# Warming transposes in two parts, another order of linear attention's products, and a price on repeated reads

## The chip, the cores and the metric

The kernel runs on one core of a Trainium2 chip. What is measured is the device time of one execution in microseconds, as the median of several runs. Its engines are TensorE (PE in the rows; its weight loads are PEld), VectorE (DVE), ScalarE (ACT), GpSimd (POOL) and SyncE (SP), which starts the transfers. Each engine works off its own queue of instructions in a fixed order; where it needs what another engine makes, it waits.

## The reference

A trunk of two layers over 512 frames and 16 meta tokens of width 1024, in float32. Each layer norms its input, multiplies it by one wide matrix, runs two groups of heads, gates their outputs and multiplies them by an output matrix. The first layer has sparse attention (an indexer scores all keys, the best are picked, softmax over them) and gated linear attention; the second has retention and stick-breaking attention. What matters here is gated linear attention, in chunks of 64:

```python
bcum = jnp.cumsum(log_a, axis=3)
q_t = q * jnp.exp(bcum);  k_t = k * jnp.exp(-bcum)
att = jnp.where(causal, jnp.einsum('bhncd,bhnsd->bhncs', q_t, k_t), 0.0)
o_intra = jnp.einsum('bhncs,bhnse->bhnce', att, v)
contrib = jnp.einsum('bhncd,bhnce->bhnde', k * jnp.exp(b_last - bcum), v)
def step(S, inp):
    dec, con = inp
    return S * dec[..., None] + con, S
o_inter = jnp.einsum('bhncd,bhnde->bhnce', q_t, S_before)
return from_chunks(o_intra + o_inter)
```

Retention has the same form with a fixed decay per head. Its output is also a sum of a product of attention with values and a product of queries with the state before the chunk.

## The kernel before

The kernel doesn't issue its instructions as its code stands. It records them all (one helper, line 406, issues each of them, so every row of the trace has that line, and groups are told apart by the names of their tiles). Each recorded operation gets a price (`price`, with cases by engine and size), and `order` (from line 291) then places them one after the other: for each engine, of what is ready, it takes the operation that could start soonest, with the deadline as the second key, and notes its start and end by the plan's own clock. Constants of the class add what a hand-over between engines costs (`LAT`) and how far neighbours overlap (`OVER`). The order found in that way is the order in each queue. What runs is the same set of instructions whatever the plan's numbers are, but they may stand in another order.

A tile is a whole for the order of its uses: a write into one part of a PSUM tile waits for a read of another part that was recorded ahead of it.

At the start, `consts` (line 675) makes the identity on GpSimd, and 46 transposes of it (`WARM`, line 496) go into one PSUM tile, `y`, whose contents nobody reads. `load_x` (line 737) loads the input in blocks, takes the sum of squares of each, and makes from the norm weights, loaded into `mid`, the tile `gains` by a transpose and a copy on ScalarE. The norm's scale is an exponential of a logarithm on tiles called `tiny`; a block `pt` is scaled by it, turned, and split into a high and a low part (`hh`, `hl`), as are the weights (`raw` to `wh`, `wl`). Three products `hh wh`, `hl wh`, `hh wl` summed in `acc` make one product of full precision.

In the first layer, the in-projection, the indexer's scores, the top-k search and four heads of gated linear attention (`gla_steps`, line 1340) share the time from about 80 to 197 us. The search runs on VectorE in rounds of a maximum of eight (MAX8) and a replacement (MATCH_REPLACE8) over rows `lt` of 272, 400 and 528 keys. A head of linear attention makes an attention tile `att` (masked from PSUM), turned keys `kt`, a small tile `m` (an `x` in the rows) for the meta tokens, with the masked copy `attm` and the copy `ktm` of their turned keys, then the state in seven steps on VectorE (`st<-st,lt,x`), and the output into a `y` tile: for each of four blocks one product of attention and values (`y<-gv,wt`) and one of queries and state (`y<-st,st`). Retention (`retention_steps`, from line 1570) ends in the same way.

Of the kernel before, what the change touches and what calls it, by code (L numbers as in the profile page):

```python
# [16 lines left out]
P = 128  # L17
DM = 1024
KT = DM // P
NMETA = 16  # L20
SEQ = 512
T = NMETA + SEQ
NB = SEQ // P
# [15 lines left out]
def blk(b):  # L39
    return slice(NMETA + P * b, NMETA + P * (b + 1))  # L40
# [126 lines left out]
class Recorder:  # L167
# [48 lines left out]
    def price(self, o):  # L216
        o.mm, o.port = None, False
        n = max([x.free() for x in o.ins + o.outs] or [1])
        sbuf = not any(x.tile.psum for x in o.ins)
        scalar = 65 if any(isinstance(x, View) and x.free() == 1 for x in o.ins) and n > 1 else 0  # L220
        if o.eng == "tensor":
            lhs, rhs = (o.args[1], o.args[2]) if len(o.args) > 2 else (o.kw["lhsT"], o.kw["rhs"])
            turn = o.name == "transpose"
            plain = rhs.dtype == F32
            k, m, n = lhs.shape[0], lhs.free(), rhs.free()
            two = plain and not turn
            o.mm = (32 if k <= 32 else 64 if k <= 64 else P, plain, max(n * 0.45 * (2 if two else 1) + 4, 107 * m / P + 4) + (107 if two and n <= P else 0))
            o.cost = max(273, 170 + 0.4375 * n) if not two else 180 + 1.62 * n
        elif o.eng == "scalar":
            o.cost = (205 if sbuf else 165) + 0.83 * n + (80 if isinstance(o.kw.get("bias"), View) or isinstance(o.kw.get("scale"), View) else 0)  # L230
            if "accum_out" in o.kw:
                o.cost += 200
        elif o.eng == "vector":
            o.port = sbuf and o.name not in ("max", "match_replace")
            if o.name == "tensor_tensor_scan":
                o.cost = 144 + 2.1 * n
            elif o.name in ("tensor_scalar", "tensor_copy") and sbuf:
                o.cost = 160 + 0.52 * n + scalar
            elif o.name == "memset":
                o.cost = 100 + 0.3 * n  # L240
            else:
                o.cost = 148 + 1.05 * n + scalar
            if o.name == "tensor_tensor_reduce" or "accum_out" in o.kw:
                o.cost += 80
            if o.name == "match_replace":
                o.cost += 70
        elif o.eng == "gpsimd":
            o.cost = {"memset": 92 + 0.84 * n, "tensor_tensor": 178 + 2.17 * n}.get(o.name, 194 + 1.5 * n)
        else:
            x = o.outs[0] if o.outs else o.ins[0]  # L250
            kb = n * x.shape[0] / 256
            o.cost = kb * 3.6


    LAT = {"tensor": 55, "vector": 33, "scalar": 34, "gpsimd": 60, "sync": 27}
    OVER = {"vector": -84, "scalar": -103, "gpsimd": -60}
    SWITCH, ROWS = 80, 95
    MARGIN = 300
    STAY = 2000
# [26 lines left out]
    def order(self):  # L286
# [10 lines left out]
        wire = 0.0  # L297
        begun = {}
        result = []

        def ready(o):
            est = 0.0
# [13 lines left out]
        while left:  # L316
            best = None
            for e, xs in lists.items():
                pick = None
                base = free[e] + (last.mm[2] if e == "tensor" and last is not None else 0)  # L320
                for o in xs:
                    est = o.est
                    ok = True
                    for t in o.tiles:
                        if t.slot:
                            continue
                        k = t.kind
                        if t.at != k.next or not k.free:
                            ok = False
                            break  # L330
                        est = max(est, min(k.free)[0] + self.LAT[e])
                    if not ok:
                        continue
                    now = free[e] + (self.slot(last, o) if e == "tensor" and last is not None else 0)
                    start = max(est, now)
                    pri = o.pri
                    if e == "tensor" and last is not None:
                        pri -= self.STAY if o.mm[0] == last.mm[0] else 0
                    key = (max(est + (self.MARGIN if e == "tensor" else 0) - base, 0.0), pri)
                    if pick is None or key < pick[0]:  # L340
                        pick = (key, start, o)
                if pick and (best is None or pick[1] < best[1]):
                    best = pick
            assert best, "no instruction can be placed"
            _, start, o = best
            e = o.eng
            lists[e].remove(o)
            cost = o.cost
            if e == "vector" and o.port and begun.get("pool", (0, 0))[0] < start < begun.get("pool", (0, 0))[1] - 100:
                cost += begun["pool"][1] - start - 70  # L350
            if e == "gpsimd" and begun.get("port", (0, 0))[0] < start < begun.get("port", (0, 0))[1] - 100:
                cost += begun["port"][1] - start - 100
            end = start + cost
            if e == "vector" and o.port:
                begun["port"] = (start, end)
            ends[o] = end
            o.begin, o.end = start, end
            if e == "tensor":
                free[e], last = start, o
            elif e == "sync":  # L360
                free[e] = start + 430
                wire = end = max(wire, start + 1900) + o.cost
                if o.outs and o.outs[0].tile.whole and o.ins and o.ins[0].tile.whole:
                    end = start + 6900
                ends[o] = o.end = end
            else:
                free[e] = end + self.OVER[e]
                if e == "gpsimd":
                    begun["pool"] = (start, end)
            for t in o.tiles:  # L370
                k = t.kind
                if not t.slot:
                    t.slot = min(k.free)
                    k.free.remove(t.slot)
                    k.next += 1
            for t in o.tiles:
                t.left -= 1
                t.ends = max(t.ends, end)
                if not t.left:
                    t.kind.free.append((t.ends, t.slot[1]))  # L380
            result.append(o)
            left -= 1
            for q in o.succs:
                q.wait -= 1
                if not q.wait:
                    ready(q)
# [23 lines left out]
class Kernel:  # L410
# [82 lines left out]


    XL, XC, XN, XW, PW, PL = 2, 9, (0, 1, 1, 2), (1, 4, 7, 10, 13), 0, 0
    WARM = 46

    LAG = {"a": 5, "d": 6, "t": 1, "v": 4, "n": 9, "s": 6, "k": 11}
    TOPY = 3
# [173 lines left out]
    def consts(self):  # L673
        nc, ins = self.nc, self.ins
# [1 line left out]
        self.ident = self.cp.tile([P, P], F32, name="ident")  # L676
        make_identity(nc.core, self.ident.real)

        warm = self.pv()
        for _ in range(self.WARM):  # L680
            self.transpose(warm[:, :P], self.ident)
        self.one = self.cp.tile([P, 1], F32, name="one")
        nc.vector.memset(self.one, 1.0)
        self.eps = self.cp.tile([P, 1], F32, name="eps")
# [2 lines left out]
        self.gains = self.cp.tile([P, 18], F32, name="gains")  # L687
        self.g = self.gains[:, :16].rearrange("p (l k) -> p l k", l=2)
        self.gb = self.gains[:, 16:18]

    def late_consts(self):
        nc, ins = self.nc, self.ins
# [35 lines left out]
    def load_x(self):  # L728
        nc, ins = self.nc, self.ins
# [59 lines left out]
        t = self.tr()  # L789
        self.transpose(t[:, :18], rows)  # L790
        nc.scalar.copy(self.gains, t[:, :18])
        self.split_next()
        todo = [(g, t0, k, c) for g, t0, c in ((first, 0, self.HALVES[0]), (second, T0, self.HALVES[1]))
                for k in range(KT)]
# [545 lines left out]
    def gla_steps(self, head, r, v, gates, ep, qs, ks, kh):  # L1340
        nc = self.nc
# [17 lines left out]

        m = self.tr()  # L1360
        nc.tensor.matmul(m[:NMETA, 0:16], ks[:, :NMETA], qs[:, :NMETA], start=True, stop=True)
        nc.vector.copy_predicated(attm[:NMETA], self.tri[:NMETA, :NMETA], m[:NMETA, 0:16])
        self.transpose(m[:NMETA, 384:512], kh[:, :NMETA])
        ktm = self.ktm[head % 2][:, :64]
        nc.vector.tensor_copy(ktm[:NMETA], m[:NMETA, 384:448])
        yield self.LAG["t"]
# [21 lines left out]
        o = self.pv()  # L1388
        ov = o.rearrange("p (b e) -> p b e", b=NB)
        for b in range(NB):  # L1390
            c = slice(P * b, P * (b + 1))
            nc.tensor.matmul(ov[:, b], att[:, b], vt[:, c], start=True, stop=False)
            nc.tensor.matmul(ov[:, b], qs[:, blk(b)], ss[:, c], start=False, stop=True)
        on = self.head_norm(ov, P, False)
        yield self.LAG["n"]
        while not gates:
# [170 lines left out]
    def retention_steps(self, head, r, v, gates, q, k, qx, kz, kzm, turned):  # L1567
# [27 lines left out]
        o = self.pv()  # L1595
        ov = o.rearrange("p (b e) -> p b e", b=NB)
        for b in range(NB):
            c = slice(P * b, P * (b + 1))
            nc.tensor.matmul(ov[:, b], av[:, b], vt[:, c], start=True, stop=False)
            nc.tensor.matmul(ov[:, b], qx[:, c], ss[:, c], start=False, stop=True)  # L1600
        on = self.head_norm(ov, P, True)
        yield self.LAG["n"]
        while not gates:
# [213 lines left out]
```

## Time and profile before

| | us |
|---|---|
| median of 3 runs | 649.36 (649.32 to 649.61) |
| profiled execution | 648.98 |
| its span, first to last instruction | 647.2 |
| TensorE busy | 625.5 (97%) |
| VectorE busy | 478.3 (74%) |
| ScalarE busy | 402.2 (62%) |

The span is what the rows are counted in; 1.78 us of the profiled execution lie outside it. Busy shares are means over the whole span, and the stages differ: which engine is the bound has to be read stage by stage, and at a waiting instruction the row names what it waited for.

### The profile page before, as it was taken

What the parts mean: (1) busy time and instruction counts of PE and PEld (TensorE: products, weight loads), DVE (VectorE), ACT (ScalarE), POOL (GpSimd) and SP (SyncE); (2) the same over time, 40 slices, a digit from 0 to 9 for tenths busy, and PEclk for the clock granted to TensorE, in tenths of its full rate; (3) what the DMA queues carried; (4) which work ended last, traced back from release to release, by engine and by line L of the source; (5) the groups of instructions that cost most, each with busy time, mean ns of one, the idle gap of its engine ahead of it and who ended that gap; (6) DMA issues with size and microseconds to landing.
All of it is one profiled execution on the core that took longest, in us unless ns stands there. A gap on an engine that the chain in (4) does not pass through costs nothing.

```text
span 647.2 us, 12268 instructions
## 1 busy us (share of the span) xinstructions
PE 625.5 (97%) x4469; PEld 578.9 (89%) x4469; DVE 478.3 (74%) x1110; ACT 402.2 (62%) x904; POOL 80.5 (12%) x199
## 2 busy tenths in 40 slices
PE   7999999899899999999999999999999999999995
PEld 6879999789889999999899999889898888988884
DVE  5777799999997676769532864789945689957443
ACT  5656572352344877789643674899744699946234
POOL 5001101100000112113121210000300010400030
PEclk9899999999999999999999999999999999999999
DMA  8437323222323322112153363212322203224503
GB/s 251 93 95 227 75 64 84 57 78 68 81 65 84 100 66 83 51 50 81 50 149 101 103 208 89 60 33 85 81 82 66 81 2 113 71 79 147 162 18 130
DMA packets 91104, 59.26 MB, mean 92 GB/s; under 512 B 7314, under 2 KB 81628, under 8 KB 91044
## 3 DMA queue, kind: packets, MB, share of 16 engines
q1 hardware_dynamic: 91044, 58.48, 31.4%
q8 instruction: 35, 0.57, 0.4%
q14 instruction: 25, 0.20, 0.1%
HBM read 53.18 MB, written 6.90 MB: 93 GB/s over the span
## 4 chain that ended last, share of the span: by engine, by line
PE 71%; DVE 15%; ACT 10%; issue 3%; POOL 0%; SPq 0%; DMA 0%; DVEq 0%; ACTq 0%; POOLq 0%
PE acc L406 48%; PE x L406 15%; PE y L406 8%; ACT wt L406 6%; DVE lt L406 3%; DVE st L406 3%; DVE wl L406 2%; DVE m L406 2%; DVE wt L406 2%; ACT wh L406 1%; ACT st L406 1%; ACT pt L406 1%; ACT ptm L406 1%; DVE pt L406 1%; SPq L406 0%
## 5 line engine op out<-in xcount | busy, mean ns | idle before, releaser
L406 PE MATMUL acc<-hh,wh 128*128 128x272 f32 (+2 forms) x968 | 244.4, 313 | 2.1 <-ACT wt L406 0.7
L406 PE MATMUL acc<-hh,wl 128*128 128x272 f32 (+2 forms) x968 | 232.8, 302 | 1.9 <-DVE wl L406 1.9
L406 PE MATMUL acc<-hl,wh 128*128 128x272 f32 (+2 forms) x968 | 233.8, 303 | 0.3
L406 PEld LDWEIGHTS acc<-hh,wh 128*128 128x128 f32 x968 | 158.7, 190 | 9.6 <-ACT hh L406 1.8
L406 PEld LDWEIGHTS acc<-hh,wl 128*128 128x128 f32 x968 | 157.5, 189 | 8.1 <-DVE wl L406 2.8
L406 PEld LDWEIGHTS acc<-hl,wh 128*128 128x128 f32 x968 | 157.5, 189 | 4.5 <-DVE hl L406 1.0
L406 ACT ACTIVATE wh<-raw 128x512 fp32r<-128x512 f32 x154 | 96.0, 630 | 102.6 <-PE acc L406 90.4
L406 DVE TENSOR_TENSOR wl<-raw,wh 128x512 fp32r<-128x512 f32 x154 | 106.4, 695 | 56.0 <-ACT wh L406 50.9
L406 ACT ACTIVATE wt<-x 128x272 f32<-128x272 f32 (+3 forms) x100 | 42.5, 454 | 29.7 <-PE x L406 15.8
L406 PE MATMUL x<-st,st 128*128 128x272 f32 (+6 forms) x240 | 51.1, 290 | 0.3 <-DVE ptm L406 0.3
L406 ACT ACTIVATE wt<-wt 128x528 f32<-128x528 f32 (+3 forms) x74 | 43.0, 603 | 7.0 <-DVE wt L406 6.4
L406 PE MATMUL x<-ident,wt 128*128 128x128 f32 (+1 forms) x296 | 44.8, 274 | 0.7 <-DVE ptm L406 0.5
L406 PEld LDWEIGHTS x<-st,st 128*128 128x128 f32 (+2 forms) x240 | 37.4, 186 | 7.8 <-ACT wt L406 2.6
L406 ACT ACTIVATE wt<-wt,tiny 128x272 f32<-128x272 f32 (+6 forms) x64 | 34.6, 561 | 11.9 <-POOL tiny L406 9.5
L406 PE MATMUL y<-pt,vt 128*128 128x256 f32 (+1 forms) x288 | 39.2, 279 | 0.2 <-ACT pt L406 0.2
L406 PEld LDWEIGHTS x<-ident,wt 128*128 128x128 f32 (+1 forms) x296 | 34.2, 139 | 3.9 <-DVE ptm L406 0.8
L406 PEld LDWEIGHTS y<-pt,vt 128*128 128x128 f32 x288 | 36.5, 190 | 0.9 <-ACT pt L406 0.4
L406 ACT ACTIVATE st<-acc 64x528 fp32r<-64x528 f32 (+1 forms) x58 | 34.8, 600 | 1.2 <-DVE lt L406 0.4
L406 DVE TENSOR_TENSOR_SCAN wt<-wt,wt 128x64 f32<-128x64 f32 (+5 forms) x50 | 29.7, 631 | 0.9 <-ACT wt L406 0.7
L406 DVE TENSOR_TENSOR pt<-x,pt 128x384 fp32r<-128x384 f32 (+1 forms) x48 | 27.7, 591 | 3.5 <-ACT pt L406 3.4
L406 ACT ACTIVATE wt<-wt,one 128x528 f32<-128x528 f32 (+3 forms) x42 | 29.5, 703 | 0.3
L406 POOL COPY pm<-wt 128x16 f32<-128x16 f32 x32 | 11.6, 384 | 138.9 <-ACT wt L406 138.6
(202 smaller groups left out, 898.0 us busy)
## 6 DMA issues: line engine op xcount, KB each, us to landing
raw<-in_w_in_ab_dram SPq DMA_DIRECT2D x64, 256.0 KB, 2.8
raw<-in_w_in_cd_dram SPq DMA_DIRECT2D x56, 256.0 KB, 2.9
raw<-in_w_out_ab_dram SPq DMA_DIRECT2D x16, 256.0 KB, 2.8
raw<-in_w_out_cd_dram SPq DMA_DIRECT2D x16, 256.0 KB, 2.6
rep<-rows SPq DMA_DIRECT2D x8, 328.0 KB, 6.4
lt<-rep SPq DMA_DIRECT2D x8, 264.0 KB, 2.8
pt<-in_x_dram SPq DMA_DIRECT2D x8, 256.0 KB, 4.2
wt<-in_x_dram SPq DMA_DIRECT2D x8, 256.0 KB, 3.5
```

The source lines that it names most:

```text
L406: getattr(getattr(self.core, o.eng), o.name)(*[bind(x) for x in o.args], **{k: bind(x) for k, x in o.kw.items()})
```

## The change

Four edits. The 46 warming transposes become 26, recorded where the 46 were, and 20 recorded behind the transpose and the copy of the norm weights, with a price of 160 ns in TensorE's order. The planner adds 98 ns (VectorE) or 115 ns (ScalarE) where an instruction reads a PSUM tile that the instruction before it on that engine also read. In linear attention the transpose of the meta tokens' keys is recorded ahead of the masked copy. And in linear attention and retention the four products with values are recorded ahead of the four with the state; the first alone starts the accumulation.

```diff
@@ price
+            if turn and o.outs[0].tile.kind.tag == "y":
+                o.mm = (P, plain, 160)
@@ class
+    SAME = {"vector": 98, "scalar": 115}
@@ order
+        reads = {}
...
                     now = free[e] + (self.slot(last, o) if e == "tensor" and last is not None else 0)
+                    if e in self.SAME and reads.get(e, set()) & set(x.tile for x in o.ins if x.tile.psum):
+                        now += self.SAME[e]
                     start = max(est, now)
...
+            if e in self.SAME:
+                reads[e] = {x.tile for x in o.ins if x.tile.psum}
@@ constants
-    WARM = 46
+    WARM = 26, 20
@@ consts
-        warm = self.pv()
-        for _ in range(self.WARM):
-            self.transpose(warm[:, :P], self.ident)
+        self.warm(0)
...
+    def warm(self, i):
+        t = self.pv()
+        for _ in range(self.WARM[i]):
+            self.transpose(t[:, :P], self.ident)
@@ load_x
         self.transpose(t[:, :18], rows)
         nc.scalar.copy(self.gains, t[:, :18])
+        self.warm(1)
@@ gla_steps
+        self.transpose(m[:NMETA, 384:512], kh[:, :NMETA])
         nc.vector.copy_predicated(attm[:NMETA], self.tri[:NMETA, :NMETA], m[:NMETA, 0:16])
-        self.transpose(m[:NMETA, 384:512], kh[:, :NMETA])
...
         for b in range(NB):
-            c = slice(P * b, P * (b + 1))
-            nc.tensor.matmul(ov[:, b], att[:, b], vt[:, c], start=True, stop=False)
-            nc.tensor.matmul(ov[:, b], qs[:, blk(b)], ss[:, c], start=False, stop=True)
+            nc.tensor.matmul(ov[:, b], att[:, b], vt[:, P * b:P * (b + 1)], start=b == 0, stop=False, skip_group_check=True)
+        for b in range(NB):
+            nc.tensor.matmul(ov[:, b], qs[:, blk(b)], ss[:, P * b:P * (b + 1)], start=False, stop=True, skip_group_check=True)
@@ retention_steps
         for b in range(NB):
+            nc.tensor.matmul(ov[:, b], av[:, b], vt[:, P * b:P * (b + 1)], start=b == 0, stop=False, skip_group_check=True)
+        for b in range(NB):
             c = slice(P * b, P * (b + 1))
-            nc.tensor.matmul(ov[:, b], av[:, b], vt[:, c], start=True, stop=False)
-            nc.tensor.matmul(ov[:, b], qx[:, c], ss[:, c], start=False, stop=True)
+            nc.tensor.matmul(ov[:, b], qx[:, c], ss[:, c], start=False, stop=True, skip_group_check=True)
```

The number of instructions is the same on every engine. In the queues it stands like this. At the start, ScalarE's queue before, where `tiny` are the logarithm and exponential of a block's norm:

```order
L406 ACTIVATE wt_278,tiny_279<-pt_193 128x512
L406 COPY gains<-x_282 128x18
L406 ACTIVATE tiny_276<-tiny_276,eps 128x1
L406 ACTIVATE tiny_276<-tiny_276 128x1
L406 ACTIVATE wh_300<-raw_231 128x512
```

and after:

```order
L415 ACTIVATE wt_272,tiny_273<-pt_188 128x512
L415 ACTIVATE tiny_270<-tiny_270,eps 128x1
L415 ACTIVATE tiny_270<-tiny_270 128x1
L415 COPY gains<-x_286 128x18
L415 ACTIVATE wh_295<-raw_222 128x512
```

The copy of the gains moved behind the two small instructions of block 0. On TensorE the start after is (before, `y_157<-ident` stood 46 times in a row ahead of `mid`):

```order
L415 MATMUL y_157<-ident 128x128 x26
L415 MATMUL y_243<-ident 128x128 x16
L415 MATMUL x_286<-ident,mid_209 128x18
L415 MATMUL x_288<-ident,gv_153 128x16
L415 MATMUL x_291<-ident,gv_153 128x16
L415 MATMUL y_243<-ident 128x128 x4
L415 MATMUL x_305<-ident,gv_153 128x16
```

Of the 20 only four came to stand behind the gains' transpose. In head 0 of linear attention, VectorE's queue around the copies for the meta tokens, before (`x_1706` is the tile `m`, `lt` are the rows searched):

```order
L406 COPY_PREDICATED wt_1611<-tri,x_1662 128x512
L406 MATCH_REPLACE lt_726<-m_21_1673,lt_726 128x528
L406 MATCH_REPLACE lt_682<-m_20_1670,lt_682 128x400
L406 MATCH_REPLACE lt_671<-m_19_1664,lt_671 128x272
L406 COPY_PREDICATED attm_104<-tri,x_1706 16x16
L406 MAX m_22_1711<-lt_671 128x8
L406 TENSOR_TENSOR wl_1718<-raw_1501,wh_1704 128x512
L406 COPY ktm_108<-x_1706 16x64
```

and after (`x_1704` is `m`):

```order
L415 MATCH_REPLACE lt_683<-m_20_1688,lt_683 128x400
L415 TENSOR_TENSOR wl_1715<-raw_1503,wh_1702 128x512
L415 COPY ktm_108<-x_1704 16x64
L415 COPY_PREDICATED attm_104<-tri,x_1704 16x16
L415 MATCH_REPLACE lt_727<-m_21_1696,lt_727 128x528
L415 MATCH_REPLACE lt_672<-m_19_1682,lt_672 128x272
L415 TENSOR_TENSOR gt_1739<-acc_1597,wt_1712 128x528
```

The copy `ktm` went ahead of `attm`, and two replacements and one search behind both. In head 3 the tail of the search stood ahead of these copies:

```order
L406 MAX m_51_2578<-lt_726 128x8
L406 COPY_PREDICATED wt_2567<-tri,x_2572 128x512
L406 MATCH_REPLACE lt_726<-m_51_2578,lt_726 128x528
L406 TENSOR_SCALAR lt_726<-lt_726 128x528
L406 COPY_PREDICATED attm_105<-tri,x_2605 16x16
L406 TENSOR_TENSOR wl_2618<-raw_2335,wh_2603 128x512
L406 COPY ktm_109<-x_2605 16x64
```

and now stands among the steps of the state (`st_2626`), behind them:

```order
L415 TENSOR_SCALAR lt_683<-lt_683 128x400
L415 SCALAR_TENSOR_TENSOR st_2626<-st_2626,lt_2032,x_2637 64x128
L415 MAX m_51_2668<-lt_727 128x8
L415 SCALAR_TENSOR_TENSOR st_2626<-st_2626,lt_2032,x_2637 64x128
L415 MATCH_REPLACE lt_727<-m_51_2668,lt_727 128x528
L415 SCALAR_TENSOR_TENSOR st_2626<-st_2626,lt_2032,x_2637 64x128
L415 TENSOR_SCALAR lt_727<-lt_727 128x528
L415 SCALAR_TENSOR_TENSOR st_2626<-st_2626,lt_2032,x_2637 64x128
```

One search, two replacements and three scalars of the tail moved from ahead of `ktm` to behind it.

## Rows read from the trace of the kernel before

**Rows 1.** The page's head: busy time by engine, and the chain by engine

```profile
PE 625.5 (97%) x4469; PEld 578.9 (89%) x4469; DVE 478.3 (74%) x1110; ACT 402.2 (62%) x904; POOL 80.5 (12%) x199
...
PE 71%; DVE 15%; ACT 10%; issue 3%; POOL 0%; SPq 0%; DMA 0%; DVEq 0%; ACTq 0%; POOLq 0%
```

**Rows 2.** Timeline, start: start, duration, engine, operation, count, [idle before and releaser]

```profile
1.58 7.74 PE L406 MATMUL y<-ident 128*128 128x128 f32 x46 [1.58 <-POOL ident masks.py:199]
...
9.25 0.23 PE L406 MATMUL x<-ident,mid 18*128 18x18 f32 x1
...
9.52 0.17 ACT L406 COPY gains<-x 128x18 f32<-128x18 f32 x1 [2.13 <-PE x L406]
9.59 0.30 ACT L406 ACTIVATE tiny<-tiny,eps 128x1 f32<-128x1 f32 x1
...
9.92 0.20 ACT L406 ACTIVATE tiny<-tiny 128x1 f32<-128x1 f32 x1
...
13.06 0.39 PE L406 MATMUL acc<-hh,wh 128*128 128x272 f32 x1 [0.36 <-ACT hh L406]
```

**Rows 3.** Windows to 23.3 us, first of `y` on PE alone, with granted clock

```profile
7.00:9.00 2.00, 2.00 (x21) 1.00 1.07 316
...
14.00:20.00 6.00, 6.00 (x27) 5.14 (x26) 4.06 (x11) 1.87 (x5) 0.00 (x0) 0.50 0.63 128
...
13.00:23.30 10.30, 9.80 (x45) 7.86 (x45) 7.80 (x20) 4.93 (x16) 0.00 (x0) 0.67 0.48 111
```

**Rows 4.** Windows: length, then busy of PE, PEld, DVE, ACT, POOL; clock

```profile
80.00:190.00 110.00, 103.59 (x838) 99.23 (x836) 107.67 (x308) 47.19 (x105) 6.84 (x18) 1.00 0.28 73
190.00:219.00 29.00, 29.00 (x236) 28.24 (x234) 22.89 (x60) 16.42 (x38) 2.62 (x9) 1.00 0.35 93
```

**Rows 5.** Timeline of PE in the same stage, four of its waits

```profile
117.93 0.28 PE L406 MATMUL x<-ident,st 128*16 128x128 f32 x1 [1.41 <-DVE attm L406]
...
128.32 0.49 PE L406 MATMUL y<-st,st 128*128 128x128 f32 x2 [0.86 <-DVE st L406]
...
171.89 0.28 PE L406 MATMUL x<-ident,st 128*16 128x128 f32 x1 [2.03 <-DVE attm L406]
...
182.42 0.49 PE L406 MATMUL y<-st,st 128*128 128x128 f32 x2 [1.06 <-DVE st L406]
```

**Rows 6.** Timeline of DVE: head 0's copy and last step, then head 3's

```profile
118.80 0.20 DVE L406 COPY ktm<-x 16x64 f32<-16x64 f32 x1
...
127.93 0.34 DVE L406 SCALAR_TENSOR_TENSOR st<-st,lt,x 64x128 f32<-64x128 f32 x1
...
185.06 0.69 DVE L406 MATCH_REPLACE8 lt<-m,lt 128x528 f32<-128x528 f32 x1
...
186.86 0.36 DVE L406 TENSOR_SCALAR lt<-lt 128x400 f32<-128x400 f32 x1
187.14 0.70 DVE L406 MAX8 m<-lt 128x8 f32<-128x528 f32 x1
...
190.27 0.21 DVE L406 COPY ktm<-x 16x64 f32<-16x64 f32 x1
...
191.80 0.28 DVE L406 COPY st<-x 64x128 f32<-64x128 f32 x1 [0.64 <-PE x L406]
...
194.08 1.88 DVE L406 SCALAR_TENSOR_TENSOR st<-st,lt,x 64x128 f32<-64x128 f32 x5
```

**Rows 7.** Tile `st` on DVE (min/median/max ns), then DVE's timeline at neighbouring reads

```profile
L406 DVE SCALAR_TENSOR_TENSOR st<-acc,st x24: 683/693/710, 31.9 to 528.6; 64x512 fp32r<-64x512 f32 x16, 64x528 fp32r<-64x528 f32 x8
...
201.98 1.42 DVE L406 SCALAR_TENSOR_TENSOR st<-acc,st 64x528 fp32r<-64x528 f32 x2
...
211.35 0.44 DVE L406 CUSTOM_DVE_ANT_0 wt<-x,wt 128x272 f32<-128x272 f32 x1
...
211.72 0.30 DVE L406 CUSTOM_DVE_ANT_0 wt<-x,wt 128x144 f32<-128x144 f32 x1
```

**Rows 8.** Timeline of PE at retention's meta tokens

```profile
465.20 0.28 PE L406 MATMUL x<-ident,pm 128*32 128x128 f32 x1 [0.52 <-POOL pm L406]
```

## What was predicted

> **What bounds the kernel now.** First the page's head and its chain of waits: TensorE is busy 97% of the span and holds 71% of the chain, VectorE follows with 15% [rows 1]. So a gain has to be time in which TensorE stands, or in which its clock is low. Before 21 us both are found: the start, where nothing can be multiplied until the first block is normed and turned [rows 2], and a stretch of low clock behind it [rows 3]. After that I went by windows. From 80 to 190 us VectorE is busy 107.67 of 110 us, TensorE 103.59; from 190 to 219 us TensorE is busy all of the time and VectorE 22.89 of 29 [rows 4]. So the stage of 80 to 190 us (gated linear attention beside the top-k search) is held by VectorE, what stands behind it by TensorE, and in the list of TensorE's waits the ones of this stage end on VectorE [rows 5]. The changed statements of linear attention lie exactly there.
>
> **The change part by part: the start.** 46 warming transposes run from 1.58 to 9.32; the gains' transpose stands behind them at 9.25, the copy of the gains at 9.52, and then, on ScalarE, the logarithm and exponential of block 0's norm at 9.59 and 9.92, then the first weight split and the rest up to the first product at 13.06 [rows 2]. The new order puts four of the 46 behind the gains' transpose, and lets the logarithm and exponential go ahead of the copy. The late transposes run 21 to 2.00 us [rows 3], 0.1 us each, so the gains' transpose comes 4 x 0.1 = 0.4 us sooner. The two small instructions, 0.30 and 0.20 us long, leave the path between the copy and the weight split: at most 0.5 us, and only if their input is there by then. Both together are 0.4 to 0.9 us; I take 0.8, near the upper end, because ScalarE waited 2.13 us ahead of the copy [rows 2], which is room for both. The four transposes behind cost nothing: TensorE waits there anyway for the normed block. The price of 160 ns that the planner gives a warming transpose is a number of the plan; it runs nowhere.
>
> **The stage of 80 to 190 us.** Two waits are aimed at. In each of the four heads the turned key of the meta tokens goes into the tile from which VectorE's masked copy `attm` reads; the transpose waited for that copy, 1.41 us in the first head and 2.03 in the third [rows 5]. Its move ahead of the copy takes this wait away. The other is the last product of query and state of a head, 0.86 and 1.06 us [rows 5], which waits for the last of seven steps of the state. Putting the four products with values first doesn't shorten that: the last product still needs the last step. These four waits make 5.36 us, nearly all of the 6.41 us for which TensorE is not busy in the stage [rows 4, 5].
>
> How much comes back is VectorE's to say, since its work in the stage is the same. Follow head 0. From the copy `ktm` at 118.80 to the last step, begun at 127.93, are 9.13 us [rows 6]. In the new order VectorE makes `ktm` with one search (MAX8 of 272) and two replacements (528 and 272 wide) fewer ahead of it, estimated at 1.6 us from [rows 6], where 528 wide takes 0.69 or 0.70 and the narrower ones about in proportion, but has those between `ktm` and the last step instead, less one search of 400: about 0.7 us more there. The net is 1.6 - 0.7 = 0.9 us gained where TensorE lost 1.41 + 0.86 = 2.27. In the fourth head the exchange is larger: the last searches, replacements and scalars of the top-k, which ended ahead of its `ktm` at 190.27, come behind it. By durations (one search of 0.70, two replacements of 0.69, three scalars of about 0.36, the middle one of three widths) they are 3.16 us [rows 6]; an estimate with the overlap of neighbours is 2.8.
>
> So up to the last step of head 3, which ended at 195.96 (194.08 + 1.88) [rows 6], VectorE has nearly all its old work. It gets there sooner only by the idle time it loses, 110 - 107.67 = 2.33 us to 190 us and 0.64 ahead of the state's first copy behind that, and by what pairs of reads no longer cost. Lower end: none of the idle goes, 0. Upper end: all of it goes, 3.0, with 0.8 for the pairs (below), 3.8 us. I take 2.0, the middle: the waits that vanish are those in which the two engines stood for each other, but most of the small gaps between VectorE's instructions stay. Behind that, in 190 to 219 us, TensorE is the bound and VectorE has 29 - 22.89 = 6.1 us of room [rows 4], so what is gained isn't given back there.
>
> **The price of pairs.** The planner now adds 98 ns (VectorE) or 115 ns (ScalarE) where an instruction reads the PSUM tile that the one before it read. That alters no instruction, only the plan's clock and through it the orders: such pairs fall from 79 to 70 on VectorE and from 79 to 73 on ScalarE, counted in the two orders. What a pair loses: two `st<-acc,st` on one tile take 1.42 us where one takes 0.693 in the median, a gap of 0.03 between them, while two reads `wt<-x` overlap: the first, 0.44 long, begins at 211.35 and ends at 211.79, the second begins at 211.72 [rows 7]. So a held pair loses about 0.03 + 0.07 = 0.1 us, and nine fewer 0.8 to 0.9 us, all on engines that are waited for only in this stage; it is in the upper end above and in nothing else. The `wt` pair also reads one tile, and yet isn't held: the tile alone can't be the condition. [...]
>
> **Retention, and the rest.** Its output products are put in the same order, with the last one as late as before: 0. Around the wait at 465.20 (0.52 us, for a copy on GpSimd) the new order has products ahead of that transpose [rows 8]; I take 0.5 us off, with ends of 0.5 lost (the turned keys and values of that stage stand closer together) and 1.0 gained. Elsewhere some 200 of 4000 rows of TensorE's order differ, with no wait of a size that I could name: 0 within 0.5 either way. SyncE's queue has three exchanges in its order, all of loads that are far ahead of their use: 0.
>
> **Sum:** 0.8 + 2.0 + 0.5 = 3.3 us. The profiled execution took 648.98 us, 0.38 below the median of 649.36. From the median: 649.36 - 3.3 = 646.06, say 646.0 (645.7 by the profile).
>
> **Rivals.**
> A, the forecast: 646.0; with its own ends 644.4 to 647.6.
> [...]
> C, the waits only move. VectorE, 98% busy, ends head 3 where it did, and only the start counts: 649.36 - 0.8 = 648.6. For it: [rows 4], by which most of TensorE's waits are VectorE's work and not a matter of order.
> D, slower. The searches and replacements now between `ktm` and the last step lengthen that chain by 0.7 us in head 0 and by 2.8 - 0.64 + 0.1 = 2.3 us in head 3. If `ktm` there comes no sooner than its 190.27 [rows 6], because TensorE's transpose and not VectorE's queue sets its time, TensorE stands at the last product by 0.7 + 2.3 - 0.8 (start) = 2.2 us longer: 651.6. It decides at whether `ktm` of head 3 comes before 195.96 - (5.69 + 2.3) = 187.97. For it: the chain is longer, that is in the order. Against: the waits of three heads ahead of it are gone or shorter, 5.4 us to be had for the 2.3 needed.
> That the change doesn't do what it says is no case of weight: the order shows the moves.
>
> **How the numbers follow.** A 0.48, B 0.20, C 0.20, D 0.12. A difference of 0.2% (1.3 us: 648.06 to 650.66) is about what a measurement of this kernel can tell from no change. A and B lie below it: faster 0.69 with a little of C at its edge, 0.70; the rest of C and the inner edge of D the same, 0.19; slower 0.11. Range: from B with a little more from the clock, 643.2, to C with its other terms lost and the inner side of D, 650.2; what is beyond is D's far half and a clock that stays high all through.
>
> **What would show it.** The first product at about 12.2 instead of 13.06, with the copy of the gains behind the exponential. No wait of TensorE on `attm`; waits of about 1 us ahead of the last product with the state in heads 0 and 2; the last step of head 3 at about 193 us. The difference between the two traces should be 0.8 at 21 us and about 2.8 at 200 us. It is wrong if the low clock is shorter or longer than before (B and its opposite), if the difference at 200 us is that at 21 us (C), or if TensorE stands over 2 us at head 3's last product (D).

## The result, and the profile after

The changed kernel takes 645.0 us (643.87 to 645.3, 4 runs) where the kernel before takes 649.49: a ratio of 0.9928, interval 0.991 to 0.9945, so 4.5 us less. The forecast was 646.0, with 643.2 to 650.2 as the range. The total came out as forecast; the runs below show that the reason given for it did not.

The profiled execution took 645.03 us, its span 643.0. From its page of the profile, the two lines that answer to [rows 1], busy time and the chain by engine:

```profile
PE 624.2 (97%) x4469; PEld 578.6 (90%) x4469; DVE 479.3 (75%) x1110; ACT 400.4 (62%) x904; POOL 78.1 (12%) x199
...
PE 71%; ACT 13%; DVE 10%; issue 2%; DMA 1%; SPq 1%; POOL 1%; POOLq 0%; DVEq 0%; ACTq 0%
```

TensorE still bounds it. The start, in its timeline (to be held against [rows 2]):

```profile
6.95 0.28 ACT L415 ACTIVATE tiny<-tiny,eps 128x1 f32<-128x1 f32 x1
7.26 0.20 ACT L415 ACTIVATE tiny<-tiny 128x1 f32<-128x1 f32 x1
...
8.20 0.23 PE L415 MATMUL x<-ident,mid 18*128 18x18 f32 x1
...
8.46 0.17 ACT L415 COPY gains<-x 128x18 f32<-128x18 f32 x1 [1.00 <-PE x L415]
...
12.03 0.60 PE L415 MATMUL acc<-hh,wh 128*128 128x272 f32 x1 [0.36 <-ACT hh L415]
```

Logarithm and exponential went ahead of the copy, as the order said, and the first product came at 12.03 instead of 13.06. The windows that answer to [rows 3] and [rows 4]: length, busy PE, PEld, DVE, ACT, POOL, granted clock.

```profile
13.00:23.30 10.30, 9.96 (x45) 8.52 (x44) 7.12 (x19) 4.51 (x14) 0.00 (x0) 0.56 0.54 125
...
80.00:190.00 110.00, 106.26 (x862) 101.93 (x861) 107.44 (x309) 48.88 (x110) 6.60 (x16) 1.00 0.29 75
190.00:219.00 29.00, 28.42 (x229) 27.71 (x229) 24.31 (x66) 16.48 (x39) 3.36 (x13) 1.00 0.35 93
```

The mean clock from 13 to 23.3 us fell from 0.67 to 0.56: the stretch of low clock is longer. By windows the granted clock is 0.50 all through 13.6 to 20.4 us before, and all through 12.0 to 21.9 in the changed kernel, where a product into `acc` 272 wide takes 0.43 us at 20.90 and 0.29 at 22.00, behind the stretch. Over it most of the start's gain went. Counting the products into `acc` in the two traces, the first stands 1.04 us sooner, the one at 24 us only 0.3. From there the lead stays at 0.3 to 110 us, is 2.6 at 224 us, 3.8 at 300 us and 4.2 at the last product (all places are times in the trace of before). In the stage of 80 to 190 us TensorE is busy 106.26 instead of 103.59 us, with VectorE as busy as before. Of TensorE's waits there and just behind, these are the ones of 0.3 us and more that end on VectorE (compare [rows 5]):

```profile
127.14 0.49 PE L415 MATMUL y<-st,st 128*128 128x128 f32 x2 [1.08 <-DVE st L415]
...
149.71 0.49 PE L415 MATMUL y<-st,st 128*128 128x128 f32 x2 [0.98 <-DVE st L415]
...
178.81 0.49 PE L415 MATMUL y<-st,st 128*128 128x128 f32 x2 [1.00 <-DVE st L415]
...
194.65 0.49 PE L415 MATMUL y<-st,st 128*128 128x128 f32 x2 [0.36 <-DVE st L415]
```

No wait on `attm` is left; the last product with the state still waits, now in heads 1 and 3 too. VectorE's timeline, for [rows 6]: the copy and the last step of head 0, then of head 3.

```profile
116.94 0.20 DVE L415 COPY ktm<-x 16x64 f32<-16x64 f32 x1
...
126.75 0.34 DVE L415 SCALAR_TENSOR_TENSOR st<-st,lt,x 64x128 f32<-64x128 f32 x1
...
186.59 0.20 DVE L415 COPY ktm<-x 16x64 f32<-16x64 f32 x1
...
195.34 0.73 DVE L415 SCALAR_TENSOR_TENSOR st<-st,lt,x 64x128 f32<-64x128 f32 x2
```

The last step of head 3 ends at 196.07, where before it ended at 195.96. VectorE is there no sooner, and yet TensorE is 2.3 us further ahead behind the stage than before it (2.6 at 224 us, less the 0.3 of the start). That is the point at which my account breaks, and the experiments begin there.

### The profile page after: what moved, and what is told of

Read it like the earlier page. It is cut to its first block, busy times and chain, and to the rows that moved or that the text cites. A ratio compares the mean times of both kernels' runs of the same rounds, so it can differ in the third digit from the quotient of the medians.

```text
span 643.0 us, 12252 instructions
## 1 busy us (share of the span) xinstructions
PE 624.2 (97%) x4469; PEld 578.6 (90%) x4469; DVE 479.3 (75%) x1110; ACT 400.4 (62%) x904; POOL 78.1 (12%) x199
## 4 chain that ended last, share of the span: by engine, by line
PE 71%; ACT 13%; DVE 10%; issue 2%; DMA 1%; SPq 1%; POOL 1%; POOLq 0%; DVEq 0%; ACTq 0%
PE acc L415 50%; PE x L415 15%; ACT wt L415 8%; PE y L415 6%; DVE lt L415 3%; DVE m L415 2%; DVE st L415 2%; DVE wl L415 2%; SPq L415 1%; ACT wh L415 1%; ACT st L415 1%; ACT pt L415 1%; DMA pt<-in_x_dram 1%; DMA wt<-wt 1%; ACT ptm L415 1%
## 5 line engine op out<-in xcount | busy, mean ns | idle before, releaser
L415 ACT ACTIVATE wt<-wt 128x528 f32<-128x528 f32 (+3 forms) x74 | 44.3, 609 | 7.1 <-DVE wt L415 6.4
L415 ACT ACTIVATE wt<-wt,tiny 128x272 f32<-128x272 f32 (+5 forms) x64 | 34.8, 561 | 10.1 <-POOL tiny L415 5.8
L415 POOL COPY pm<-wt 128x16 f32<-128x16 f32 x32 | 9.2, 302 | 145.7 <-ACT wt L415 145.7
```

Source lines behind the costliest of these rows:

```text
L415: getattr(getattr(self.core, o.eng), o.name)(*[bind(x) for x in o.args], **{k: bind(x) for k, x in o.kw.items()})
```

## The experiments

My theory: linear attention's new order removes the waits on `attm` and carries most of the gain, the start some 0.8 us, the price of repeated reads next to nothing by itself. Rivals: the start carries it; the price carries it. Each edit alone, and the price taken out of the changed kernel. All ratios are to runs of the kernel before on the same chip.

**Warming alone.** Linear attention and retention are as before, and repeated reads have no price.

```diff
-    WARM = 46
+    WARM = 26, 20
```

> The kernel before with only the warming transposes in two parts. Theory (the start gives little, the order of the stage from 80 to 190 us gives most): 0.3 to 1.0 us faster than before, 648.5 to 649.2, according to how much of the sooner first product the longer stretch of low clock takes back. Rival (the start carries the gain): 645.5 to 646.5. The waits of TensorE on attm in heads 0 and 2 of linear attention should be as before, 1.4 and 2.0 us.

Measured: 0.9994 (0.9985 to 1.0003), or 0.4 us with an interval that holds 0; the medians, 648.26 and 648.98 us, differ by 0.7. In its profiled execution the first product is 0.93 us sooner and the lead stays, with a mean clock of 0.69 from 13 to 23.3 us. So the sooner start is real, but what is left of it in the time is too small to be told from nothing.

**Linear attention and retention alone.** The diff shows linear attention; retention's eight output products are put in the same order.

```diff
+        self.transpose(m[:NMETA, 384:512], kh[:, :NMETA])
         nc.vector.copy_predicated(attm[:NMETA], self.tri[:NMETA, :NMETA], m[:NMETA, 0:16])
-        self.transpose(m[:NMETA, 384:512], kh[:, :NMETA])
...
-            nc.tensor.matmul(ov[:, b], att[:, b], vt[:, c], start=True, stop=False)
-            nc.tensor.matmul(ov[:, b], qs[:, blk(b)], ss[:, c], start=False, stop=True)
+            nc.tensor.matmul(ov[:, b], att[:, b], vt[:, P * b:P * (b + 1)], start=b == 0, stop=False, skip_group_check=True)
+        for b in range(NB):
+            nc.tensor.matmul(ov[:, b], qs[:, blk(b)], ss[:, P * b:P * (b + 1)], start=False, stop=True, skip_group_check=True)
```

> The kernel before with only the order of linear attention's and retention's products changed (the transpose ahead of the masked copy, the products with values first); warming and prices as before. Theory: it takes most of the gain, 2.3 to 3.5 us faster, 646.0 to 647.2, since the waits on attm go. Rival (the price of repeated reads makes the gain, by a plan that knows where VectorE is): no more than 1 us faster, 648.4 or above.

Measured: 1.0008 (0.9996 to 1.0019), nothing. TensorE's timeline in this kernel shows where the waits went:

```profile
115.49 0.28 PE L413 MATMUL x<-ident,st 128*16 128x128 f32 x1
...
119.02 0.43 PE L413 MATMUL x<-vmz,ktm 128*64 128x128 f32 x2 [1.55 <-DVE attm L413]
...
128.22 0.49 PE L413 MATMUL y<-st,st 128*128 128x128 f32 x2 [0.93 <-DVE st L413]
...
161.45 0.66 PE L413 MATMUL x<-ident,wt 128*128 128x128 f32 x4 [3.06 <-DVE wt L413]
```

The transpose no longer waits (115.49, no bracket), but the next user of VectorE's copies does, for 1.55 us, about as long as the transpose did in [rows 5]: in head 0 the wait was moved by one instruction. The wait of head 2 is gone as well, but ahead of it the transposes of a head's normed output (`wt`, made on VectorE) now wait 3.06 us, where before they waited for nothing. My theory falls here.

**The price alone, and the changed kernel without it.** In the first, the prices of 98 and 115 ns are added to the kernel before and nothing else; in the second, the changed kernel has

```diff
-    SAME = {"vector": 98, "scalar": 115}
+    SAME = {"vector": 0, "scalar": 0}
```

> The kernel before with only the price of repeated reads. Theory: the waits on attm stay in some form, and the time is within 1 us of before, 648.4 to 650.4. Rival (the price makes the gain): 2 us or more faster, 647.4 or below.

> The changed kernel with both prices of repeated reads at 0. Theory: it keeps at least 3 of the 4.5 us gained, 645.0 to 646.5. Rival (the price makes the gain): 647.5 or above.

Measured: 0.9937 (0.9925 to 0.9949), 645.02 us, for the price alone: all of the changed kernel's gain within the intervals. 1.0001 (0.999 to 1.0011) for the changed kernel without it: no gain. The price is both enough and needed, and the three other edits together can't be told from nothing without it. In the profiled execution of the kernel without the price a part of that is the clock's: behind a wait of 3.05 us that ended at 160.28, at the place of the 3.06 above, the granted clock was 0.50 from 160.8 to 164.2 us.

```profile
160.80:164.20 3.40, 3.40 (x18) 3.40 (x17) 3.37 (x9) 0.60 (x1) 0.00 (x0) 0.50 0.47 134
```

Pairs of products into `acc` take 0.64 us there instead of 0.41, so by an estimate from these rows it costs 3.4 x (1 - 0.41 / 0.64) = 1.2 us, less than a third of the gain that is missing.

Why numbers that no engine executes save 4 us is seen when the plan's own start of each VectorE instruction is set beside the trace, as the lead of the plan, which is how much earlier the plan has an instruction than the trace (instructions of both are in the same order, 1015 of them):

```
lead of the plan over the trace, us      at 81 us   at 186 to 191   growth
kernel before                              4.83         12.60         7.8
changed kernel                             4.56          9.82         5.3
price alone                                4.96          9.83         4.9
```

In the stage where VectorE has no room (busy 107.67 of 110 us), the plan of before got 7.8 us further ahead of it. So it told TensorE to come for results that weren't there, and held back the plain products that could have run in the meantime. In the kernel with the price alone the transpose of head 0 stands behind eight more of them (569 products into `acc` instead of 561), in TensorE's timeline at the place of the first line of [rows 5]:

```profile
117.56 0.28 PE L413 MATMUL x<-ident,st 128*16 128x128 f32 x1
...
80.00:190.00 110.00, 106.54 (x857) 101.66 (x855) 107.68 (x309) 48.55 (x107) 6.81 (x17) 1.00 0.30 74
```

It begins at nearly the same time as before (117.93), but without a wait: TensorE did other work first. The second line is the window of the stage: as much TensorE time as in the changed kernel.

**Which price.** If a truer plan is the cause, a still truer one must give more. Aligned with the trace of before, the condition of the change marks 74 instructions, and not all of them are held, that is, begin only behind the end of the one ahead. In [rows 7] the two `st<-acc,st`, the second of which begins 14 ns behind the first, read and write different halves of the partitions, and the two `wt<-x,wt`, which overlap by 73 ns, both start at the first partition. So I tried a condition by the partitions on the trace: marked as held is an instruction whose operand starts in another quarter of the partitions than the last read or write of that memory. Counted over the trace of before (start of an instruction less the end of the one ahead; those that begin more than 60 ns behind it wait for something else and are left out):

```
by the quarter   on the same tile   count   median ns   10% to 90%
not held         no                  631      -81        -84 to -12
not held         yes                  25       34        -82 to 35
held             no                  123       31         31 to 33
held             yes                  49       14         13 to 35
```

The trace of before agrees with this condition: all 172 instructions that it calls held begin behind the one ahead, by 13 to 44 ns, and those of the first row overlap it by 81 ns in the median. The 25 of the second row look like an exception: 15 of them begin 33 to 35 ns behind. But each of these 15 waits for a semaphore that only VectorE raises, so for a result of its own; the other ten overlap by 71 to 85 ns, although they read the same tile. The condition of the change misses 123 of 172, among them the seven steps of the state in each of the first three heads, which go back and forth between the halves of the partitions: there the gap to the plan was 116 ns each. From 80 to 190 us 78 of VectorE's 258 instructions are held; against the plan they begin 7.9 us later in sum, and all the others together 0.5. That accounts for the 7.8 us of the table. So I priced VectorE by that condition, and left ScalarE's price as it was.

```diff
-                    if e in self.SAME and reads.get(e, set()) & set(x.tile for x in o.ins if x.tile.psum):
+                    if e == "vector":
+                        now += 110 if self.held(o, side) else 0
+                    elif e in self.SAME and reads.get(e, set()) & set(x.tile for x in o.ins if x.tile.psum):
                         now += self.SAME[e]
...
+    def held(self, o, last):
+        if any(last.get(("r", x.tile.psum), self.quad(x)) != self.quad(x) for x in o.ins):
+            return True
+        return any(last.get(("w", x.tile.psum), self.quad(x)) != self.quad(x) for x in o.outs[:1])
```

> The changed kernel with another condition for VectorE's price: 110 ns where an operand starts in another quarter of the partitions than the last read or write of that memory did, and nothing for the same tile alone; ScalarE's price stays. Aligned with the trace of before, that condition marks all the instructions of VectorE that begin after the end of the one ahead (172 of them, 14 to 31 ns behind it), the tile alone only 74. Theory now (the gain comes from a plan that knows when VectorE is there): at least as fast as the changed kernel, 643.0 to 645.2. Rival (any shift of the plan's numbers gives another order, and this one was lucky): anywhere from 645.5 to 650.

Measured: 641.29 us, 0.9874 (0.9859 to 0.989), 3.7 us below the changed kernel. Its windows, and TensorE and VectorE in its timeline at head 0's last product:

```profile
80.00:190.00 110.00, 109.78 (x897) 105.93 (x896) 106.60 (x301) 50.01 (x110) 6.09 (x15) 1.00 0.29 74
190.00:219.00 29.00, 29.00 (x240) 28.84 (x238) 27.04 (x74) 19.13 (x43) 5.97 (x14) 1.00 0.39 102
...
124.75 0.40 PE L436 MATMUL y<-st,st 128*128 128x128 f32 x2
126.96 0.49 PE L436 MATMUL y<-st,st 128*128 128x128 f32 x2
...
126.56 0.34 DVE L436 SCALAR_TENSOR_TENSOR st<-st,lt,x 64x128 f32<-64x128 f32 x1
```

TensorE is busy 109.78 of 110 us. VectorE's last step ends at 126.90, as late as in the changed kernel (126.75 + 0.34 = 127.09), but the product that needs it now stands at 126.96, without a wait, behind plain products. VectorE's work of the stage went partly into the room of the next one (27.04 of 29 us there, 22.89 in [rows 4]). The plan's lead grows from 3.78 at 80 us to 4.72 at 191: 0.9 us instead of 7.8. Not all of what is won is kept: the products into `acc` are 10.8 us ahead of the kernel before at 224 us and 8.3 at 290, and TensorE now waits 3.2 us in five places for `pm` from GpSimd.

**Sum or place.** A rival: only the sum of added time matters, or any shift draws another order and this one was lucky. Four kernels against that. Two spread the time evenly over all instructions of the kernel before, one takes the same away, and one changes the size of the price by held instructions.

```diff
 8 and 11 ns more      +    OVER = {"vector": -76, "scalar": -92, "gpsimd": -60}
 33 and 11 ns more     +    OVER = {"vector": -51, "scalar": -92, "gpsimd": -60}
 8 and 11 ns less      +    OVER = {"vector": -92, "scalar": -114, "gpsimd": -60}
 changed, 130 ns       +                        now += 130 if self.held(o, side) else 0
```

> The kernel before, with about the same sum of added time spread evenly: every VectorE instruction 8 ns longer in the plan, every ScalarE instruction 11 ns, no price on pairs. In the stage of 80 to 190 us that is 258 x 8 = 2.1 us against 28 x 98 = 2.7 us by pairs. Theory with the place of the price deciding: less than half of the gain, 647.2 to 649.4. Theory with only the sum deciding: 645.5 to 647.

> The kernel before with every VectorE instruction 33 ns longer in the plan and every ScalarE instruction 11 ns, no price on pairs: in the stage of 80 to 190 us 258 x 33 = 8.5 us, as much as the 78 held instructions there at 110 ns make. Theory (the sum of the plan's time decides, not where it is put): 641 to 643, as with the price by held instructions. Rival (where it is put decides): 644 or above, waits of TensorE on the masked copy or the state remaining.

> The kernel before with every VectorE instruction 8 ns and every ScalarE instruction 11 ns shorter in the plan, the opposite of the kernel with 8 and 11 ns more, which ran at 0.994 of before. Theory (the plan was too fast, and added time helps because it comes nearer to the trace): 649 or above, no gain. Rival (any shift of the plan's numbers gives another order, and a gain of 3 us is within what such a draw gives): 647.5 or below is possible, with waits gone at other places.

> The changed kernel with the price by held instructions at 130 ns instead of 110. Theory (a plan near the trace is good, and near it the time is flat): 640.5 to 642.5. Rival (each order is a draw, and 641.3 was a lucky one): off by 2 us or more, 643.3 or above.

Measured: 8 ns more 645.37 us, 0.994 (0.9928 to 0.9953); 33 ns more 646.79, 0.9966 (0.9954 to 0.9978); 8 ns less 651.51, 1.0049 (1.0036 to 1.0063); 130 ns 639.95, 0.9859 (0.9845 to 0.9873). For the small amount the place didn't matter: spread evenly it gives what the pairs give, against my expectation. For the large amount it does. 33 ns on all put as much time into the stage (258 x 33 = 8.5 us) as 110 ns on the held ones (78 x 110 = 8.6). Beside the kernel that has that price and no edit by hand either (642.24 us, below) they give 4.6 us less. And the direction is right: time taken away costs. The stage of 80 to 190 us in the kernel with 33 ns more and in the one with 8 ns less, as windows, with the first kernel's longest wait and the second's:

```profile
80.00:190.00 110.00, 108.10 (x873) 103.41 (x872) 105.86 (x303) 49.73 (x110) 6.18 (x15) 1.00 0.30 75
...
PE x L406 <- POOL pm L406: 2.1, 1, 2.1
```

```profile
80.00:190.00 110.00, 102.27 (x822) 97.84 (x821) 107.43 (x306) 45.40 (x102) 6.95 (x18) 1.00 0.29 72
...
PE x L406 <- DVE attm L406: 4.3, 2, 2.4
```

Even time fills the stage to 108.10, better than the change, and gives much of it back: its products are 5.2 us ahead of the kernel before at 224 us and 1.8 at 234, and between these lies the wait of 2.1 us on `pm`, in sparse attention at 229.07. With time taken away the waits on `attm` grow to 4.3 us. Counted as in the table above, the plan's lead grows by 9.4 us with 8 ns less, 5.8 with 8 ns more, 2.6 with 33 and 0.1 with 130 ns on the held ones. TensorE's busy time in the stage goes the other way: 102.27, 105.77, 108.10 and 109.78 us. The kernel at 130 ns shows no drop beside the one at 110, so the 641.29 was no lucky single draw; that it is another 1.3 us lower goes in part with the clock (its two runs with a mean of 0.996 took 639.2 us, the two with 0.991 took 640.7 and 641.0), and its own share isn't told apart.

**The parts that remain.** VectorE's price alone on the kernel before; the changed kernel with the 46 transposes in one row; the price by held instructions without any edit by hand.

> The kernel before with the price on VectorE's pairs alone. Theory (the stage bound by VectorE carries the gain): 644.5 to 646.0, as with both prices. Rival (ScalarE's price has a share): 647 or above.

> The changed kernel with the 46 warming transposes in one row again. Theory: the split is worth little, as alone, and the order of the rest stays: 0 to 1 us slower than the changed kernel, 644.8 to 646.2. Rival (the split shifts the whole plan and is needed for the gain): 647 or above.

> The kernel before with the price by held instructions (110 ns) on VectorE and by tile on ScalarE, and neither the two parts of the warming nor the new order of products. Theory (the plan makes the gain, the edits by hand add little): 640.5 to 642.5. Rival (the order of products is worth 2 us or more once the plan is true): 643.5 or above.

Measured, the first: 646.31, 0.9953 (0.9941 to 0.9966), so VectorE's price makes some three quarters of what both prices make, a little less than expected, though the intervals overlap. At 224 us both kernels are about equally far ahead (2.6 and 2.4 us), so in these two executions what ScalarE's price adds comes behind the stage. The second: 645.5, 0.9946 (0.9934 to 0.9959), the same as the changed kernel within the intervals. The third: 642.24, 0.9892 (0.9879 to 0.9906), beside 0.9874 (0.9859 to 0.989) with the edits by hand: these are worth about 1 us together, with intervals that just overlap.

## Why the prediction was right, and where it was wrong

The time lies 1.0 us below the forecast and inside its range. That it came so near is partly luck: between the two profiled executions the start gave 0.5 us less than its term, the stage 0.3 more and the rest 1.1 more, and the edit that carries the gain stood in the sum with nothing of its own. Point by point:

**The start, 0.8 us.** The first product came 1.04 us sooner [rows 2 against 12.03]. The term failed one step later: I counted it as kept. It is 0.3 us at 24 us, behind a longer stretch of low clock (0.50 through 12.0 to 21.9 us, 13.6 to 20.4 before); a longer stretch of low clock stood among the signs of being wrong and had no price. Rival B, a shorter stretch of low clock, went the other way in the profiled run (a mean of 0.56 instead of 0.67), and no run shows the time from the clock that the lower end of the range, 643.2, is built on: with the warming alone the mean was 0.69, and the time came to 0.4 us less with an interval that holds 0.

**The stage, 2.0 us.** The size held (2.3 us), the reason didn't. The step that failed is "how much comes back is VectorE's to say". I took VectorE at 98% for a bound of the stage, and so counted only its idle time and its held pairs. It wasn't one: its last step of head 3 ended at 196.07 and not at 193, and TensorE gained all the same, since the order gave it other work to do until then. With the price by held instructions TensorE is busy 109.78 of 110 us with VectorE at 106.60. The question for this stage was not how soon VectorE is done, but whether the order of TensorE knows how late it is. The other failed step is the transpose moved ahead of the copy: alone it moved the wait of head 0 to the next instruction, and another of 3.06 us came up elsewhere. That is rival C's mechanism: without the price the waits only move.

**The price, 0 by itself.** This is the step that was most wrong: "That alters no instruction, only the plan's clock and through it the orders" was true, and yet the orders that it makes got no term; only the pairs that run less often did, inside the upper end of the stage. It is the whole gain, within the intervals. The error could have been seen in the profile of before: the waits of [rows 5] all end on VectorE, in a kernel whose order comes from a plan that was meant to avoid them.

**The condition of a held pair.** I had read from [rows 7] that the tile alone can't be the condition, and yet counted the pairs by the tile. The quarter of the partitions fits the trace better: all 172 that it marks begin behind the one ahead, while of the 74 marked by the tile ten overlap by 71 to 85 ns. As a price it was worth 3.7 us more.

**Retention and the rest, 0.5 us.** From 224 to 300 us the lead grew by 1.2 us and by some 0.4 behind that; I had 0.5. Two short waits went (0.16 at 225.06 and 0.25 at 254.07 in the trace of before), and the wait for `pm` shrank. In the kernel that `pm` is written by stick-breaking attention, not by retention as the heading of [rows 8] has it:

```profile
455.15 0.29 PE L415 MATMUL x<-ident,pm 128*32 128x128 f32 x1 [0.24 <-POOL pm L415]
```

But a second such wait, of 0.17 us, came at 556.5, and two of 0.25 and 0.27 us on VectorE's `st` at 423.4 and 524.8, so in sum these waits make nothing of the 1.6 us. TensorE's busy time over the span is 624.2 us instead of 625.5 ([rows 1] and above), so a part of it is products that take less time in the new order; which, wasn't tried and stays open.

**Rival D** is refused: `ktm` of head 3 came at 186.59, before the 187.97 that I gave as the point of decision. Its chain did get longer, 9.5 us from `ktm` to the end of the last step instead of 5.7: 3.8 us where 2.3 were priced.

## What to carry to other kernels

Where a planner sets the order, compare its start times with the trace, engine by engine, before moving code by hand: the stage in which its lead grew, by 7.8 us, was here the one in which it sent TensorE to wait. An engine that is busy 98% of a stage is not for that reason its bound (TensorE's busy time here rose from 103.59 to 109.78 of 110 us, with VectorE's at 107.67 and 106.60); ask what of its work is needed only later, and whether the engine that waits has other work that could stand first. A wait that is taken away at one instruction should be looked for at the next user of the same data (1.41 us at the transpose in head 0 became 1.55 us at the product with `ktm`).

## What the runs showed of the hardware

In the trace of the kernel before, the 631 instructions of VectorE that neither the quarter nor the tile marks overlap the one ahead by 81 ns in the median, and the 172 that the quarter of the partitions marks begin 13 to 44 ns behind it, 131 of them without a wait on VectorE's own semaphore. The tile alone doesn't go with it: the ten that read the same tile, aren't marked by the quarter and aren't held up by a result of VectorE overlap by 71 to 85 ns.

Two waits of TensorE of some 3 us had different clocks behind them. Behind 3.05 us in the changed kernel without the price the granted clock was 0.50 from 160.8 to 164.2 us; behind 3.06 us at nearly the same place in the kernel with linear attention's order alone it stayed at 1.00, the mean from 80 to 190 us.

The low clock behind the start varied between kernels: the mean from 13 to 23.3 us was 0.67 before, with the first product at 13.06, 0.56 in the changed kernel, with it at 12.03, 0.69 with the warming alone, and in the one at 130 ns 0.83:

```profile
13.00:23.30 10.30, 9.35 (x52) 7.50 (x51) 8.69 (x23) 5.81 (x18) 0.00 (x0) 0.83 0.56 132
```

Of the 1.04 us gained ahead of this stretch in the changed kernel 0.3 were left at 24 us, so such a gain needs timed runs and not one profile.
